# A hybrid decoder layer: the embedding's projection dealt to three handovers, low weights behind the last addition, fewer sums, seven end tiles by TensorE

## The chip, the cores and the metric

The kernel runs on one core of a Trainium2 chip. The metric is the device time of one execution in microseconds (us). A profiled execution also gives a span, from its first to its last instruction, to which all times of a timeline refer.

The engines are named as the profile names them: PE is TensorE (PEld its weight loads), DVE is VectorE, ACT is ScalarE, POOL is GpSimd, and SP is SyncE, whose queue issues all DMAs here.

## The reference

One layer of a decoder is computed for 256 prompt tokens and 8 single-token samples, all in 32-bit floating point, with model width 2048 and feed-forward width 5632:

```python
h = h + 0.5 * rmsnorm(swiglu(rmsnorm(h, g1), w1_gate, w1_up, w1_down), g1_post)
mix, cb, xb, hs = token_mixer(rmsnorm(h, g_mix), ...)     # w_in -> conv group | SSD group -> w_out
h = h + rmsnorm(mix, g_mix_post)
h = h + 0.5 * rmsnorm(swiglu(rmsnorm(h, g2), w2_gate, w2_up, w2_down), g2_post)
gate = sigmoid(rmsnorm(h, g_ple) @ w_ple_gate)
h = h + rmsnorm(gate * (p @ w_ple_proj), g_ple_post)
```

`rmsnorm(x, g)` is `x * rsqrt(mean(x*x) + 1e-6) * g`. The token mixer has an input projection, a conv group (1024 channels, 31 taps), an SSD group (48 heads, 8 groups, state 128) and an output projection. The product `p @ w_ple_proj`, with `p` of width 256, does not depend on `h`; it is called the embedding's projection here.

## The kernel before, in words

**Layout.** Activations lie transposed: 128 channels on the partitions, T = 264 columns (256 prompt, 8 samples) along them. The width 2048 is 16 such tiles (KD). A weight block is 128x128.

**Products.** One 32-bit product is made of three matmuls in a shorter format (`mm3`, L277 to L279): high weights by the high part of the activation, high weights by its low part, low weights by its high part. So each activation tile is split in a high part (written by ACT) and a low part (DVE: value minus high part; tile `act`). Each weight half unit of up to 8 blocks comes by one DMA from SP (`wraw`), is cast by ACT (`whi`, L172), and its rest is taken by DVE (`wlo`, L175). There are 4 buffers of each. A table, `PLAN`, lists the weight units in the order of use; `Weights.next` loads two units ahead of the one in use (`AHEAD`), and a unit has one or two halves.

**Stages in order.** FFN 1; handover 1; the in-projection and the mixer; the out-projection; handover 2; FFN 2; handover 3; the gate's GEMM of the embedding; the tail. A handover is the stretch between the last matmul of one stage and the first of the next: the last output tile is added to its sum (`y`, 16 tiles), squared, and the squares are summed over channels by a matmul with ones (L339, tile `ps`); ACT makes the reciprocal root by Ln and Exp (`rr`); DVE updates `h` tile by tile (`residual`) and splits each into the next stage's input. The squares of the first 14 tiles or so are added up along the way in a tile `run`, the last ones go into TensorE by themselves (`SumSq`, `direct` says how many).

**First GEMM of a stage** (`gemm_first`): to start while the input is still being made, 7 or 8 output columns are accumulated side by side, one input tile after another. The first seven matmuls of an input tile need its high part alone. The later columns are done one by one (`gemm_one`).

**Handover 1** issues the embedding's projection: 16 output columns of two blocks each, 96 matmuls, in two weight units; ACT copies each column out (`pp`, L615) and SP stores it in DRAM (`pproj`), from where the last stage loads it. Handovers 2 and 3 issue `HANDOVER = (4, 11)` matmuls on an identity whose result is not used (`warm`, L379): 4 ahead of the last sum and 11 behind it.

**Handover 1's extra sums.** There the norm of the updated `h` is taken before `h` exists, from three sums: of y squared, of h times y (`hy`) and of y squared with gains (`yy`).

**The mixer** sends scan values through DRAM: `rows` to `d_bc`, and back as `cbc`, broadcast over the partitions; DVE multiplies the sample states with `cbc` (L241).

**The tail** makes `h + e * scale` for the 16 tiles: five tiles by TensorE (identity times h, plus identity times the scaled e, copied by ACT), four by POOL, the rest by DVE, and stores them.

**Order.** A scheduler orders the instructions of each engine; `tc.high_priority`, `tc.issue_after` and `tc.keep_in_program_order` bind it. Engines take their instructions in that order. The diff's lines in the code after are numbered otherwise: L277 to L279 become L302 to L304, L339 becomes L363, L241 and L244 become L266 and L269, L175 becomes L185.

## Time and profile before

| | us |
|---|---|
| median of 3 runs (lowest to highest) | 2396.03 (2394.15 to 2398.36) |
| the profiled execution | 2395.91 |
| its span | 2394.1 |
| PE busy | 2365.5 |
| DVE busy | 1579.9 |
| ACT busy | 1185.8 |
| FFN 1 ends, handover 1 begins (PE) | 769.8 |
| out-projection ends, handover 2 begins | 1513.4 |
| FFN 2 ends, handover 3 begins | 2281.2 |
| last matmul of the gate's GEMM | 2379.8 |

The granted TensorE clock was 0.996 over the span. A timeline row reads: start, duration, engine, line, operation, output tile and inputs, shape, count, and in brackets how long the engine had been idle and what released it. Rows of like instructions that follow each other are drawn together ("x8"), with the duration of the whole group. A matmul on 32-bit operands (the sums, the warm ones) leaves two records. A window row has us, busy time and count of PE, PEld, DVE, ACT and POOL, the granted clock, the DMA share and GB/s.

### The profile page before, as it was taken

The page shows a single profiled execution, that of the slowest core. Times are in us where ns is not written, and L with a number is a line of the kernel's source. Part 1 is how long each engine was busy: PE and PEld are TensorE (multiplying, and loading weights), DVE is VectorE, ACT ScalarE, POOL GpSimd, SP SyncE. Part 2 cuts the span into 40 slices and gives each one's busy share as a digit, 9 for nine tenths or more (in the row PEclk, how much of TensorE's full clock was granted, in tenths as well). Part 3 has the DMA queues.
Part 4 walks back from the last instruction along what each step waited for, and adds up shares of the span by engine and source line. Part 5 has one row for each costly group of instructions (what it writes and reads, how often), then busy time and mean ns, then how long its engine had stood idle before and what let it go on. Part 6 is the DMA issues. An engine that isn't in the chain of part 4 may idle for free.

```text
span 2394.1 us, 47473 instructions
## 1 busy us (share of the span) xinstructions
PE 2365.5 (99%) x19540; PEld 2345.8 (98%) x19540; DVE 1579.9 (66%) x2380; ACT 1185.8 (50%) x1786; POOL 183.3 (8%) x201
## 2 busy tenths in 40 slices
PE   9999999999999989999999999999999999999998
PEld 9999999999999988999999999999999999999998
DVE  7554455545557978989898965866545665565586
ACT  6444444434456565566665455644444443344465
POOL 1400000000004000000000021010100000000103
PEclk9999999999999999999999999999999999999999
DMA  7665555565556766666665556467666676666563
GB/s 259 217 185 184 183 182 183 185 183 182 183 172 190 261 212 203 212 218 216 221 215 175 184 175 230 160 229 242 233 212 227 237 235 220 217 229 214 180 206 134
DMA packets 163434, 489.89 MB, mean 205 GB/s; under 512 B 25312, under 2 KB 43024, under 8 KB 163216
## 3 DMA queue, kind: packets, MB, share of 16 engines
q1 hardware_dynamic: 163216, 486.85, 62.8%
q8 instruction: 153, 2.51, 0.4%
q14 instruction: 65, 0.53, 0.1%
HBM read 465.65 MB, written 22.42 MB: 204 GB/s over the span
## 4 chain that ended last, share of the span: by engine, by line
PE 92%; DVE 3%; DMA 2%; issue 1%; ACT 1%; SPq 0%; POOL 0%; ACTq 0%; DVEq 0%; POOLq 0%
PE acc L277 29%; PE acc L279 29%; PE acc L278 29%; PE ps L277 1%; PE ps L278 1%; DVE wlo L175 1%; PE ps L279 1%; DMA d_bc<-rows 1%; DMA cbc<-d_bc 1%; ACT whi L172 1%; DMA wraw<-in_w 1%; DVE h L241 0%; PE ps L339 0%; DVE h L244 0%; PE ps L880 0%
## 5 line engine op out<-in xcount | busy, mean ns | idle before, releaser
L279 PE MATMUL acc<-act,wlo 128*128 128x264 f32 x6128 | 1735.5, 285 | 7.9 <-DVE wlo L175 7.8
L278 PE MATMUL acc<-act,whi 128*128 128x264 f32 x6128 | 1721.2, 282 | 0.0
L277 PE MATMUL acc<-act,whi 128*128 128x264 f32 x6128 | 1705.7, 282 | 7.6 <-DVE h L244 4.3
L175 DVE TENSOR_TENSOR wlo<-wraw,whi 128x1024 fp32r<-128x1024 f32 (+2 forms) x814 | 977.6, 1203 | 576.4 <-ACT whi L172 574.3
L172 ACT CAST whi<-wraw 128x1024 fp32r<-128x1024 f32 (+2 forms) x814 | 832.0, 1024 | 970.9 <-PE acc L278 689.5
L277 PEld LDWEIGHTS acc<-act,whi 128*128 128x128 f32 x6128 | 1149.9, 189 | 10.7 <-DVE h L244 4.4
L279 PEld LDWEIGHTS acc<-act,wlo 128*128 128x128 f32 x6128 | 1146.8, 187 | 10.7 <-DVE wlo L175 9.4
L278 PEld LDWEIGHTS acc<-act,whi 128*128 128x128 f32 x6128 | 1148.9, 187 | 1.5 <-issue 0.5
L241 POOL TENSOR_TENSOR run<-run,tmp 128x264 f32<-128x264 f32 x77 | 72.3, 939 | 887.3 <-ACT tmp L268 886.8
L244 DVE SCALAR_TENSOR_TENSOR y<-v,vec,y 128x255 f32<-128x255 f32 (+26 forms) x240 | 107.6, 471 | 0.7
L241 POOL TENSOR_TENSOR s<-s,eap 128x1024 f32<-128x1024 f32 x24 | 49.1, 2046 | 626.7 <-DMA s<-in_hst 554.0
L244 DVE SCALAR_TENSOR_TENSOR s<-bb,xds,s 128x128 f32<-128x128 f32 x192 | 52.6, 346 | 59.9 <-POOL s L241 59.9
L241 DVE TENSOR_TENSOR tmp<-acc,rr 128x264 f32<-128x264 f32 x99 | 42.5, 430 | 50.7 <-PE acc L279 50.7
L286 ACT CAST act<-tmp 128x264 fp32r<-128x264 f32 x104 | 42.0, 411 | 53.1 <-DVE tmp L241 51.4
L241 DVE TENSOR_TENSOR tmp<-tmp,acc 128x264 f32<-128x264 f32 x84 | 35.9, 428 | 40.0 <-PE acc L279 39.5
L241 POOL TENSOR_TENSOR run<-run,y 128x264 f32<-128x264 f32 x7 | 9.5, 1350 | 590.3 <-ACT run L321 514.5
L241 DVE TENSOR_TENSOR act<-tmp,act 128x264 fp32r<-128x264 f32 x120 | 54.2, 455 | 0.5 <-ACT act L286 0.5
L278 PE MATMUL ps<-act,whi 128*128 128x264 f32 x192 | 52.3, 283 | 0.0
L279 PE MATMUL ps<-act,wlo 128*128 128x264 f32 x192 | 52.1, 284 | 0.0
L268 ACT ACTIVATE tmp<-tmp 128x264 f32<-128x264 f32 x112 | 47.0, 420 | 7.3 <-DVE tmp L241 7.0
L268 ACT ACTIVATE tmp<-y 128x264 f32<-128x264 f32 x67 | 28.0, 425 | 44.6 <-DVE y L241 43.3
L241 DVE TENSOR_TENSOR y<-y,acc 128x264 f32<-128x264 f32 x80 | 34.0, 425 | 23.9 <-PE acc L279 23.8
(172 smaller groups left out, 1037.6 us busy)
## 6 DMA issues: line engine op xcount, KB each, us to landing
wraw<-in_w SPq DMA_DIRECT2D x755, 512.0 KB
h<-in_hst SPq DMA_DIRECT2D x24, 512.0 KB
s<-in_hst SPq DMA_DIRECT2D x24, 512.0 KB
out_nss<-s SPq DMA_DIRECT2D x24, 512.0 KB
wraw<-in_w SPq DMA_DIRECT2D x35, 256.0 KB
wraw<-in_w SPq DMA_DIRECT2D x23, 384.0 KB
ab<-d_cs SPq DMA_DIRECT2D x16, 384.0 KB
cbc<-d_bc SPq DMA_DIRECT2D x8, 512.0 KB
```

The costliest lines, as they stand in the source:

```text
L172: self.hi = nc.scalar.copy(hi[:, c:d], raw[:, c:d]).ins
L175: nc.vector.tensor_tensor(out=lo[:, c:d], in0=raw[:, c:d], in1=hi[:, c:d].bitcast(F32), op=ALU.subtract)
L241: return (eng or nc.vector).tensor_tensor(out=out, in0=in0, in1=in1, op=op)
L244: return nc.vector.scalar_tensor_tensor(out=out, in0=in0, scalar=scalar, in1=in1, op0=op0, op1=op1)
L268: i = nc.scalar.activation(out=out, in_=in_, func=func, bias=bias, scale=scale)
L277: nc.tensor.matmul(acc, hi, x[:, 0, :], start=first, stop=False)
L278: nc.tensor.matmul(acc, hi, x[:, 1, :], start=False, stop=False)
L279: traced[0] = nc.tensor.matmul(acc, lo, x[:, 0, :], start=False, stop=last).ins
L286: nc.scalar.copy(t[:, 0, :], x)
```

## The change

1. The embedding's 16 columns are dealt out by `PP = (8, 12)`: 8 at handover 1, 4 at handover 2, 4 at handover 3, each as one weight unit of the plan. They are issued in a fixed order with the sums: one column between the sum of `run` and the last sum, the others behind it. The warm matmuls of the handovers are gone. `p` is loaded and split again for handovers 2 and 3. The last four columns are copied straight to the tiles where they are used; 12 go through DRAM.
2. Low weights: some subtractions are deferred (`defer`, `later`) and issued later (`flush`): the second half of the next stage's first unit behind the last addition, its second unit behind the second residual and behind a split inside `update_input` (`load_late`).
3. Six sums (L339) fewer: a constant is added into `run`, and three `SumSq` give no square to TensorE by itself. The sum of a first GEMM is pinned ahead of its last input tile.
4. The first input tile of the stages behind handovers 2 and 3 is made from y with the product of two gains (`both`), high and low part on DVE; h's first tile is updated later.
5. `hy` and `yy` take the gain as a factor, so y need not be scaled first.
6. In the tail seven tiles go by TensorE, the last DVE pair is done as single tiles, stores are by pair, and the first three identity products stand between the two sums.

```diff
-HANDOVER = (4, 11)
+PP = (8, 12)
...
+    def embed(lo, hi):
+        plan.append(("pp", [0, 1], list(range(lo, hi))))
...
-    for q in range(2):
-        plan.append(("pp", [0, 1], list(range(8 * q, 8 * q + 8))))
+    embed(0, PP[0])
...
+    embed(PP[0], PP[1])
     ffn(2)
+    embed(PP[1], KD)
...
+                    def low(lo=lo[:, c:d], raw=raw[:, c:d], hi=hi[:, c:d]):
+                        self.lo = keep(
+                            nc.vector.tensor_tensor(out=lo, in0=raw, in1=hi.bitcast(F32), op=ALU.subtract)
+                        ).ins
+
+                    if a >= defer:
+                        self.later.append(low)
+                        continue
...
+    def flush(self, behind):
+        with self.tc.issue_after(behind), self.tc.high_priority(offset=1000):
+            self.later.popleft()()
+
+    def load_late(self, after):
+        self.after = after
+        self.load(defer=0)
+        self.after = None
...
-        def total(self, behind=None, idle=(0, 0)):
-            d = ps_tile([P, P]) if idle[0] else None
+        def total(self, behind=None, keep=lambda ins: ins, between=None):
             p = ps_tile([P, T])
             with tc.issue_after(behind) if behind is not None else nullcontext():
                 for i, s in enumerate(self.parts):
                     last = i == len(self.parts) - 1
-                    if last and idle[0]:
-                        warm(idle[0], d)
-                    m = nc.tensor.matmul(p, ones, s, start=i == 0, stop=last)
-            if idle[1]:
-                tc.keep_in_program_order(m)
-                warm(idle[1], d)
+                    if last and between:
+                        between()
+                    keep(nc.tensor.matmul(p, ones, s, start=i == 0, stop=last))
...
+                    if m == KD - 1 and ws.later:
+                        ws.flush(i.ins)
                     done(m, ys[m])
+                    if m == 2:
+                        ysq.add_plain(eq)
...
+    def embed(lo, hi, out, **how):
+        w = ws.next(**how)
+        for m in range(lo, hi):
+            acc = acc_tile()
+            for i in range(2):
+                mm3(acc, w[i * (hi - lo) + m - lo], pacts[i], i == 0, i == 1, tc.keep_in_program_order)
+            out(m, acc)
+            yield m
+
+    def ysq_total(ysq, cols):
+        return ysq.total(traced[0], tc.keep_in_program_order, lambda: next(cols))
...
-    ysq, hy, yy = (SumSq(KD, f"run{i}", ep, urgent=not i) for i in range(3))
+    ysq, hy, yy = (
+        SumSq(n, f"run{i}", ep, urgent=not i, direct=d) for i, n, d in ((0, KD + 1, 1), (1, KD, 0), (2, KD, 1))
+    )
...
-        tt(t, H(m), y, ALU.mult)
+        stt(t, y, gain, H(m), ALU.mult, ALU.mult)
...
-    def update_input(rs, post, pre):
-        xs, sq = [], SumSq(KD, eng=nc.vector)
+    def update_input(rs, stage):
+        post, pre = GAINS[stage]
+        xs, sq, made = [], SumSq(KD, eng=nc.vector, direct=0), []
         with tc.high_priority():
-            for k in range(5):
-                if k < 4:
-                    residual(k, ys[k], rs, post, tc.keep_in_program_order)
-                if k:
-                    xs.append(split(H(k - 1), V(pre, k - 1), tc.keep_in_program_order))
+            t, x, u = tmp(), act_tile(), tmp()
+            keep_order(stt(t, ys[0], both[:, stage : stage + 1], rs, ALU.mult, ALU.mult))
+            keep_order(stt(x[:, 0, :], H(0), V(pre), t, ALU.mult, ALU.add))
+            keep_order(stt(u, H(0), V(pre), t, ALU.mult, ALU.add))
+            keep_order(tt(x[:, 1, :], u, x[:, 0, :].bitcast(F32), ALU.subtract))
+            xs.append(x)
+            for k in range(1, 5):
+                residual(k % 4, ys[k % 4], rs, post, lambda i: made.append(keep_order(i).ins))
+                if k == 2:
+                    ws.flush(made[-1])
+                if k > 1:
+                    xs.append(split(H(k - 1), V(pre, k - 1), lambda i: made.append(keep_order(i).ins)))
+                if k == 3:
+                    ws.flush(made[-1])
...
+    cols = embed(PP[1], KD, lambda m, acc: nc.scalar.copy(e4[m // 4][:, m % 4, :], acc), fill=False)
+    rs = ffn_scale(ysq, cols)
+    ws.load_late(order["last"])
+    for _ in cols:
+        pass
+    xs, sq = update_input(rs, 1)
...
-TAIL_VECTOR = [(0, 2), (2, 1), (3, 1), (4, 2), (6, 2), (8, 2), (10, 2)]
-TAIL_TENSOR = [0, 1, 2, 4, 5]
+TAIL_VECTOR = [(0, 2), (2, 1), (3, 1), (4, 2), (6, 2), (8, 2), (10, 1), (11, 1)]
+TAIL_TENSOR = [0, 1, 2, 4, 5, 6, 7]
```

Where instructions stand, first on VectorE at handover 3. `wlo_0` and `wlo_8` are the two halves of a weight unit's low part, `y` the last addition, `act` the low part of an input tile. Before:

```order
L241 TENSOR_TENSOR y_21725<-y_21725,acc_27354 128x264
L175 TENSOR_TENSOR wlo_8_27363<-wraw_8_27361,whi_8_27362 128x768
L175 TENSOR_TENSOR wlo_0_27410<-wraw_0_27408,whi_0_27409 128x1024
L241 TENSOR_TENSOR y_21788<-y_21788,acc_27407 128x264
L175 TENSOR_TENSOR wlo_8_27416<-wraw_8_27414,whi_8_27415 128x768
L244 SCALAR_TENSOR_TENSOR tmp_27483<-y_20819,vec,rr_27460 128x264
L241 TENSOR_TENSOR h_17895<-h_17895,tmp_27483 128x264
L244 SCALAR_TENSOR_TENSOR tmp_27486<-y_20882,vec,rr_27460 128x264
L241 TENSOR_TENSOR h_17895<-h_17895,tmp_27486 128x264
L244 SCALAR_TENSOR_TENSOR act_27489<-h_17895,vec,act_27489 128x264
```

The same place in the change (the first unit's halves are 27370 and 27376, the second unit's 27443 and 27448):

```order
L185 TENSOR_TENSOR wlo_0_27370<-wraw_0_27368,whi_0_27369 128x1024
L266 TENSOR_TENSOR y_21745<-y_21745,acc_27367 128x264
L185 TENSOR_TENSOR wlo_8_27376<-wraw_8_27374,whi_8_27375 128x768
L269 SCALAR_TENSOR_TENSOR tmp_27475<-y_20776,both,rr_27427 128x264
L269 SCALAR_TENSOR_TENSOR act_27476<-h_17814,vec,tmp_27475 128x264
L269 SCALAR_TENSOR_TENSOR tmp_27477<-h_17814,vec,tmp_27475 128x264
L266 TENSOR_TENSOR act_27476<-tmp_27477,act_27476 128x264
...
L185 TENSOR_TENSOR wlo_0_27443<-wraw_0_27441,whi_0_27442 128x1024
L269 SCALAR_TENSOR_TENSOR act_27489<-h_17814,vec,act_27489 128x264
...
L185 TENSOR_TENSOR wlo_8_27448<-wraw_8_27446,whi_8_27447 128x768
```

The second unit's low weights stood ahead of the last addition and behind it, all before the first tile; now the first unit's stand there, and the second unit's are among the input tiles.

Second, TensorE at handover 1 in the change: the end of the FFN (`acc_8959`), then sums and embedding columns (`acc_9016`, `acc_9069`):

```order
L304 MATMUL acc_8959<-act_8055,wlo_8_8848 128x264
L363 MATMUL ps_9014<-run_8108,ones 128x264
L302 MATMUL acc_9016<-act_9007,whi_0_8901 128x264
...
L304 MATMUL acc_9016<-act_9010,wlo_8_8908 128x264
L363 MATMUL ps_9014<-tmp_8997,ones 128x264
L363 MATMUL ps_9030<-run_8114,ones 128x264
L363 MATMUL ps_9030<-tmp_9002,ones 128x264
L363 MATMUL ps_9033<-run_8112,ones 128x264
L302 MATMUL acc_9069<-act_9007,whi_0_8901 128x264
```

Before, the six sums were spread among the columns; now five stand close together around the first column.

Third, VectorE in the mixer's first group. Before, two low-weight subtractions stood ahead of the two `cbc` products:

```order
L175 TENSOR_TENSOR wlo_0_10164<-wraw_0_10162,whi_0_10163 128x1024
...
L175 TENSOR_TENSOR wlo_8_10170<-wraw_8_10168,whi_8_10169 128x1024
...
L241 TENSOR_TENSOR h_478_9922<-h_478_9922,cbc_9920 128x1024
L241 TENSOR_TENSOR h_479_9924<-h_479_9924,cbc_9920 128x1024
```

In the change one of the two stands behind them:

```order
L185 TENSOR_TENSOR wlo_0_10083<-wraw_0_10081,whi_0_10082 128x1024
...
L266 TENSOR_TENSOR h_466_9841<-h_466_9841,cbc_9839 128x1024
L266 TENSOR_TENSOR h_467_9843<-h_467_9843,cbc_9839 128x1024
L185 TENSOR_TENSOR wlo_8_10089<-wraw_8_10087,whi_8_10088 128x1024
```

The second half of a weight unit moved behind the products that wait for `cbc`.

167 lines of the change are left out of this document (90 added, 77 removed).

## The prediction

> **What bounds the kernel now.** I read the page first (busy shares and the clock row), then the waits of TensorE, then timelines of TensorE, VectorE and ScalarE around the three handovers, the mixer's first group and the tail.
>
> ```profile
> PE 2365.5 (99%) x19540; PEld 2345.8 (98%) x19540; DVE 1579.9 (66%) x2380; ACT 1185.8 (50%) x1786; POOL 183.3 (8%) x201
> PE acc L279 <- DVE wlo L175: 7.8, 6, 4.2
> PE acc L277 <- DVE h L244: 4.3, 1, 4.3
> PE acc L277 <- ACT whi L172: 3.0, 3, 2.5
> 1517.20:1552.80 35.60, 35.40 (x296) 35.21 (x295) 35.39 (x73) 23.22 (x44) 0.00 (x0) 1.00 0.50 161
> ```
>
> TensorE is busy 99%, so what it issues is what the kernel costs. The window row (us, then busy and records of PE, PEld, DVE, ACT, POOL, then clock) gives the price: 35.6 / 296 = 0.120 us per matmul. It also holds the trap: in that window, which is the first GEMM after handover 2, VectorE is busy 35.39 of 35.6 us. There a matmul saved is worth nothing if VectorE is later. Only about 24 us of the span are TensorE waits; the waits rows name the largest, all in the mixer.
>
> **Handover 1.** Today all 16 embedding columns (96 matmuls) stand there.
>
> ```profile
> 769.75 0.28 PE L279 MATMUL acc<-act,wlo 128*128 128x264 f32 x1
> 771.78 0.71 PE L339 MATMUL ps<-run,ones 128*128 128x264 f32 x2 [0.22 <-POOL run L241]
> 770.65 1.98 POOL L241 TENSOR_TENSOR run<-run,tmp 128x264 f32<-128x264 f32 x2 [2.09 <-ACT tmp L268]
> 772.59 1.79 POOL L241 TENSOR_TENSOR run<-run,hy 128x264 f32<-128x264 f32 x1
> 783.44 0.43 DVE L241 TENSOR_TENSOR act<-tmp,act 128x264 fp32r<-128x264 f32 x1
> 786.26 0.43 DVE L241 TENSOR_TENSOR act<-tmp,act 128x264 fp32r<-128x264 f32 x1
> 770.00:785.50 15.50, 14.94 (x109) 13.93 (x108) 11.42 (x19) 13.07 (x31) 3.73 (x3) 1.00 0.73 244
> ```
>
> The last FFN matmul starts at 769.75; the window is filled with 109 records until 785.5, where the in-projection effectively begins. The change leaves 8 columns there: 48 x 0.12 = 5.76 us go. Its order now puts the sum of run directly behind the last FFN matmul. That sum waits for POOL as it does today (771.78), with nothing in front, so TensorE idles 1.9 us. Then one column (0.72), and the sums of tmp, yy and hy in a fixed order. The last of these can start when POOL's hy addition ends, 772.59 + 1.79 = 774.4. It costs 0.44 us (below), seven columns 42 x 0.12 = 5.04: 779.9. The first input column is then ready, so the in-projection starts near 780.1 in place of 785.5: **-5.4 us**. VectorE makes one input column every 786.26 - 783.44 = 2.82 us there, TensorE uses one in 24 x 0.12 = 2.88. The lead shrinks but does not vanish. If it did, 16 tiles at a little over 2.88 would cost up to 1 us; if the sums' waits hide better, 0.5 more is won: between -4.4 and -5.9.
>
> **Handovers 2 and 3.** Each loses 15 warm matmuls and gets four columns, 24 x 0.12 = 2.88 us.
>
> ```profile
> 1513.42 0.29 PE L279 MATMUL acc<-act,wlo 128*128 128x264 f32 x1
> 1513.55 0.61 PE L339 MATMUL ps<-run,ones 128*128 128x264 f32 x2
> 1513.99 1.05 PE L379 MATMUL ps<-ident,ones 128*128 128x128 f32 x8
> 1514.45 0.42 DVE L241 TENSOR_TENSOR y<-y,acc 128x264 f32<-128x264 f32 x1
> 1515.44 0.71 PE L339 MATMUL ps<-tmp,ones 128*128 128x264 f32 x2 [0.40 <-ACT tmp L268]
> 1515.99 2.62 PE L379 MATMUL ps<-ident,ones 128*128 128x128 f32 x22
> 1517.24 0.49 DVE L244 SCALAR_TENSOR_TENSOR tmp<-y,vec,rr 128x264 f32<-128x264 f32 x1 [1.50 <-ACT rr L268]
> 1518.81 0.51 PE L277 MATMUL acc<-act,whi 128*128 128x264 f32 x2 [0.20 <-ACT act L268]
> 1560.72 0.39 PE L277 MATMUL ps<-act,whi 128*128 128x264 f32 x1 [0.42 <-DVE rr L421]
> ```
>
> A sum costs 1513.99 - 1513.55 = 0.44 us. The last matmul starts at 1513.42, but the addition that needs it waits for a low-weight subtraction and starts at 1514.45. In the change that subtraction stands behind the addition, which then starts a third of a us behind the last matmul (its 0.29 and the signal), near 1513.75: 0.7 us. The first input tile now comes from VectorE alone (two of its instructions, then the tile is there) instead of two on VectorE and one on ScalarE (1517.24 to 1518.81): 0.55 us more. The columns (2.88) and both sums (0.88) fit under this chain. The GEMM starts near 1517.6, **1.2 us earlier**; handover 3 shows the same steps:
>
> ```profile
> 2281.21 0.29 PE L279 MATMUL acc<-act,wlo 128*128 128x264 f32 x1
> 2282.24 0.42 DVE L241 TENSOR_TENSOR y<-y,acc 128x264 f32<-128x264 f32 x1
> 2284.93 0.49 DVE L244 SCALAR_TENSOR_TENSOR tmp<-y,vec,rr 128x264 f32<-128x264 f32 x1 [1.40 <-ACT rr L268]
> 2286.49 0.51 PE L277 MATMUL acc<-act,whi 128*128 128x264 f32 x2
> 2291.35 0.49 DVE L244 SCALAR_TENSOR_TENSOR tmp<-y,vec,rr 128x264 f32<-128x264 f32 x1
> 2291.76 1.22 DVE L175 TENSOR_TENSOR wlo<-wraw,whi 128x1024 fp32r<-128x1024 f32 x1
> 2292.89 0.43 DVE L241 TENSOR_TENSOR run<-run,tmp 128x264 f32<-128x264 f32 x1
> 2293.24 0.49 DVE L244 SCALAR_TENSOR_TENSOR tmp<-y,vec,rr 128x264 f32<-128x264 f32 x1
> 2294.79 0.95 DVE L175 TENSOR_TENSOR wlo<-wraw,whi 128x768 fp32r<-128x768 f32 x1
> 2295.66 0.43 DVE L241 TENSOR_TENSOR run<-run,tmp 128x264 f32<-128x264 f32 x1
> 2326.32 0.61 PE L339 MATMUL ps<-run,ones 128*128 128x264 f32 x2
> ```
>
> The GEMM starts near 2285.2 instead of 2286.49 (-1.3). But then VectorE, already full, gets more to do: the embedding's unit takes a place of the two-unit lookahead, so both halves of the second unit's low weights (two subtractions) and the extra operations of the first tile land inside its chain. Start to start the rows give 0.405 (scalar_tensor_tensor, 2291.35 to 2291.76), 1.13 (1024 wide), 0.35 (tensor_tensor, 2292.89 to 2293.24) and 0.87 (768 wide, 2294.79 to 2295.66). In the new order the low half of the fifth input tile is VectorE's 29th instruction, at either handover: 15 x 0.405 + 9 x 0.345 + 3 x 1.135 + 2 x 0.87 = 14.3 us after the chain's start, today's 1517.24 (2284.93) less the 0.7 = 1516.55 (2284.24), hence at 1531.0 (2298.7). TensorE, 7 columns x 3 x 0.12 = 2.52 us per tile, asks for it after four tiles and the seven matmuls that need only the high half: 1517.6 + 10.08 + 0.84 = 1528.5 (2296.1). So it **stalls 2.5 us**, and 0.2 more at the next tile; the later tiles catch up. One sum of the two at the end of this GEMM goes (0.44). Handover 2: 1517.6 + 16 x 2.52 + 0.44 + 2.7 = 1561.0, against 1560.72, and the constant that column 7 waits for today (0.42 in its row) comes no earlier, since its ScalarE work stands behind a weight cast; with 1 us for that it is **+1.3**, between -2.4 (no stall) and +2.1. Handover 3: 2285.2 + 40.32 + 0.44 + 2.7 = 2328.7, against 2286.49 + 40.32 + 0.88 = 2327.7: **+1.0**, between -1.7 and +2.
>
> **Fewer sums.** Two are gone in the first FFN, one in the second, on TensorE's path and with nothing waiting: 3 x 0.44 = **-1.3**. The others (hy, the two behind update_input) are in the figures above.
>
> **The mixer** is untouched in code, but the scheduler's order moved.
>
> ```profile
> 861.78 0.85 SPq L826 DMA_DIRECT2D cbc<-d_bc  x1
> 869.18 2.36 DVE L241 TENSOR_TENSOR h<-h,cbc 128x1024 f32<-128x1024 f32 x2 [4.61 <-DMA cbc<-d_bc]
> 876.25 0.59 PE L279 MATMUL acc<-act,wlo 128*128 128x264 f32 x1 [4.19 <-DVE wlo L175]
> 872.00:876.20 4.20, 0.06 (x1) 0.00 (x0) 4.20 (x7) 0.79 (x1) 0.00 (x0) 0.52 0.39 123
> 876.20:878.00 1.80, 1.75 (x8) 1.75 (x9) 1.80 (x3) 1.30 (x2) 0.00 (x0) 0.50 0.73 259
> 878.00:880.00 2.00, 2.00 (x11) 2.00 (x11) 2.00 (x5) 1.99 (x5) 0.00 (x0) 0.50 0.74 297
> ```
>
> VectorE stands at the cbc products 4.61 us for their DMA, and low weights queue behind. In the change one more half unit of low weights stands behind them (its 1.13 us and the products' 2.36 come ahead of a tile that TensorE needs sooner), but one weight load of 512 KB less is ahead of the DMA chain that feeds cbc. If cbc lands 2.5 us earlier, TensorE resumes about 1 us earlier than 876.25; if it lands as today, 1.5 us later. The seven later groups have smaller shifts. I take **0**, between -3 and +4.
>
> The stall of 4.19 us is followed by a granted clock of 0.50 (last two rows): a long stall is paid twice. The Trainium skill states this rule ("TensorE: Matmul & The Clock Gate", Part 1: after about 3.4 us without work TensorE runs at half rate until it has been busy as long again), and this trace agrees with its 0.50. By that rule taking the warm matmuls away speaks against the change; the idle that I count in the handovers (1.9 us at most) and the 2.5 us stalls are shorter than the 4.19 that is seen to do it, so the sum has no such loss, and it is a rival below.
>
> **Tail.**
>
> ```profile
> 2389.86 0.70 DVE L241 TENSOR_TENSOR h<-h,prod 128x528 f32<-128x528 f32 x1
> 2388.07 2.88 SPq L1186 DMA_DIRECT2D out_y<-h  x6
> ```
>
> The chain sum, Ln, Exp, products stays. VectorE's list gets two tiles shorter and its last two pairs become single tiles; at the 0.43 of a single tile's addition it ends some 0.5 us before today's 2389.86 + 0.70 = 2390.56, and the last store is half as large, but stores queue on SP (six in 2.88 us). **-0.3**, between -0.6 and +0.2.
>
> **Sum.** -5.4 + 1.3 + 1.0 - 1.3 + 0 - 0.3 = -4.7 us. The profiled execution took 2395.9 (span 2394.1 and 1.8 around it), 0.1 below the median of 2396.03; so 2391.2 to 2391.3, and I say **2391.2 us**. A change under 0.2%, 4.8 us, cannot be told from none here; the forecast lies on that border.
>
> **The rivals.**
> (a) VectorE keeps up in both GEMMs: the stalls fall away. For it: later tiles have slack, and a stall on TensorE also delays the casts. Against it: 35.39 of 35.6 us busy today. It gives 2391.2 - 2 x 2.7 = 2386 us. Chance 0.25.
> (b) The handover's gain is spent again: the in-projection becomes bound by VectorE. Its 2.82 us against 2.88 leave 0.06 a tile; If the weight casts, which share ScalarE with these tiles, come 0.3 us later per tile, 16 tiles cost about 4.5: 2395.7. Chance 0.15.
> (c) On the other side: the cbc products, moved ahead of low weights in all eight groups. From the point where cbc is not earlier than today, each group holds TensorE for one more subtraction, 1.13 us, and in the first one longer: 8 x 1.13 + 1 = 10: 2401.3 us, slower. For it: the waits row of 7.8 us on low weights shows that path live. Against it: the DMA chain is shorter. Chance 0.08.
> (d) The clock halves in handovers 2 and 3. A half-rate stretch as long as the one seen (876.2 to 880 and a little more) loses about 2 us each: 2391.2 + 4 = 2395.2. Chance 0.04.
> The forecast with its own range, 2388.5 to 2394.5, keeps 0.48; half of that lies below 2391.2.
>
> **The numbers.** Faster by over 0.2%: all of (a) and half of the forecast, 0.25 + 0.24 = 0.49. Slower by over 0.2%: (c) and a little of (b), 0.10. The rest, 0.41, is within 0.2%. The range goes from full gain, 2385.5, to just over (b) and (d), 2397: one in ten is left out above, less below.
>
> **What would show it.** TensorE's first in-projection matmul about 10.3 us behind the last FFN matmul, where 15.75 lie today; a wait of 2 to 3 us of TensorE for VectorE's input tiles (act) near 14 us after the start of each VectorE chain, where today there is none; first GEMMs that start 4.1 us behind the last matmul in place of 5.4; no half-rate clock in the handovers; the wait on cbc in the first group within 2.5 us of 4.61. The forecast is wrong if that act wait is missing, if the in-projection's first GEMM shows waits for VectorE, or if the mixer's stalls sum to more than 4 us away from today's.

## The result, and the profile after

The changed kernel took **2403.86 us** (median of 9 runs, 2400.64 to 2408.05), the kernel before on the same chip 2397.3 (9 runs, 2394.15 to 2399.92): a ratio of 1.0028, 95% interval 1.0018 to 1.0038. It is **slower by 0.28%**, where 2391.2 us was forecast; 2403.86 lies outside the range. Its profiled execution is the fastest of the nine: 2400.64 us, span 2398.9, against 2395.91 and 2394.1 before. The profiles of two experiments below (the state term first, and the products later) fell on disturbed executions and are not read.

The table gives stretches of TensorE's timeline, cut at the start of the first or last matmul of each. (In the kernel before, six matmuls of the embedding stand among the first ones of the in-projection, which begin at 784.78; there the cut is put at 785.51, so that the first GEMM has its own 384 matmuls as in the other columns.) "Again" is a second profile of the changed kernel; the last four columns are experiments told below.

| us | before | after | again | padded | sixteen | three edits | among sums |
|---|---|---|---|---|---|---|---|
| FFN 1 | 769.75 | 769.05 | 768.58 | 768.48 | 770.15 | 768.74 | 768.65 |
| handover 1 | 15.76 | 9.30 | 9.36 | 15.45 | 17.40 | 17.32 | 16.32 |
| first GEMM of the in-projection | 45.96 | 47.19 | 47.11 | 46.06 | 45.96 | 45.96 | 46.17 |
| rest of in-projection, mixer, out-projection | 681.95 | 684.76 | 687.72 | 682.82 | 677.34 | 675.00 | 677.60 |
| handover 2 | 5.38 | 4.20 | 4.20 | 4.20 | 4.94 | 4.94 | 4.94 |
| first GEMM of FFN 2 | 41.21 | 44.03 | 44.07 | 44.02 | 41.96 | 42.02 | 41.98 |
| up to column 7 | 0.70 | 2.10 | 2.09 | 2.09 | 2.09 | 1.23 | 1.24 |
| rest of FFN 2 | 720.49 | 722.49 | 723.48 | 721.38 | 721.64 | 720.03 | 720.03 |
| handover 3 | 5.28 | 4.11 | 4.10 | 4.10 | 4.94 | 4.94 | 4.94 |
| first GEMM of the gate | 41.21 | 44.08 | 45.41 | 45.43 | 41.94 | 41.95 | 41.93 |
| rest of the gate | 52.09 | 53.18 | 52.72 | 51.84 | 53.18 | 52.72 | 52.72 |
| tail | 14.32 | 14.44 | 16.13 | 14.59 | 16.62 | 14.33 | 14.34 |

Handover 1 gave 6.46 us and handovers 2 and 3 gave 1.2 each, and more than all of it was lost in the stretches behind them. First the page of the changed kernel and the waits of its TensorE (us in total, times, longest):

```profile
PE 2364.3 (99%) x19476; PEld 2342.3 (98%) x19476; DVE 1577.8 (66%) x2394; ACT 1186.6 (49%) x1790; POOL 185.1 (8%) x206
```

```profile
PE acc L304 <- DVE wlo L185: 9.9, 5, 7.3
PE ps L930 <- DVE xde L266: 3.8, 2, 2.4
PE acc L303 <- DVE act L269: 3.8, 4, 1.6
PE acc L302 <- DVE h L269: 3.3, 1, 3.3
PE ps L302 <- DVE rr L442: 1.8, 1, 1.8
```

TensorE issues 64 records less and is busy 1.2 us less, yet the span is 4.8 longer. Three rows are new or much larger: `act` is the stall that was forecast for the two GEMMs, `rr` is column 7's constant (0.4 us before), and `xde` is a wait in the mixer that the prediction did not name (0.7 us in the kernel before). The row of `wlo` holds one wait of 7.3 us, where the longest was 4.2.

Handover 1 on TensorE (last FFN matmul, first sum, the last sums, first input column):

```profile
769.05 0.29 PE L304 MATMUL acc<-act,wlo 128*128 128x264 f32 x1
770.06 0.71 PE L363 MATMUL ps<-run,ones 128*128 128x264 f32 x2 [0.72 <-POOL run L266]
...
772.72 0.71 PE L363 MATMUL ps<-run,ones 128*128 128x264 f32 x2
...
778.35 0.28 PE L302 MATMUL acc<-act,whi 128*128 128x264 f32 x1
```

From 769.05 to 778.35 are 9.30 us. The first sum waits 0.72 us and not the 1.9 of the forecast.

The mixer's first group (near 865) and second group (near 935): VectorE, then TensorE, then three windows of TensorE's clock (PEclk, the third number from the end):

```profile
863.79 2.36 DVE L266 TENSOR_TENSOR h<-h,cbc 128x1024 f32<-128x1024 f32 x2 [7.99 <-DMA cbc<-d_bc]
866.07 1.22 DVE L185 TENSOR_TENSOR wlo<-wraw,whi 128x1024 fp32r<-128x1024 f32 x1
...
933.04 1.22 DVE L185 TENSOR_TENSOR wlo<-wraw,whi 128x1024 fp32r<-128x1024 f32 x1
934.18 0.55 DVE L266 TENSOR_TENSOR xde<-xdt,dte 128x384 f32<-128x384 f32 x1
934.65 1.22 DVE L185 TENSOR_TENSOR wlo<-wraw,whi 128x1024 fp32r<-128x1024 f32 x1
...
936.54 0.55 DVE L266 TENSOR_TENSOR xde<-xdt,dte 128x384 f32<-128x384 f32 x1
```

```profile
867.34 0.59 PE L304 MATMUL acc<-act,wlo 128*128 128x264 f32 x1 [7.30 <-DVE wlo L185]
...
934.88 0.88 PE L930 MATMUL ps<-xde,rr 128*128 128x384 f32 x2 [2.37 <-DVE xde L266]
937.24 1.62 PE L930 MATMUL ps<-xde,rr 128*128 128x384 f32 x2 [1.48 <-DVE xde L266]
```

```profile
867.00:871.00 4.00, 3.66 (x16) 3.66 (x17) 4.00 (x9) 0.65 (x1) 0.00 (x0) 0.50 0.48 136
903.00:909.00 6.00, 3.53 (x16) 3.54 (x17) 6.00 (x21) 3.00 (x11) 0.00 (x0) 0.50 0.77 249
935.00:941.00 6.00, 4.52 (x23) 2.63 (x24) 4.64 (x10) 2.22 (x6) 0.00 (x0) 0.72 0.71 226
```

VectorE stands 7.99 us for `cbc`, where it stood 4.61, and the half of low weights that TensorE needs is the next instruction behind it. TensorE resumes 88.99 us after the in-projection's start (867.34 less 778.35); before it was 876.25 less 785.5, 90.75, so this stall by itself lost nothing. The `xde` waits near 935 did: up to there the two kernels run even, behind them the changed one is 5 us later by the starts of equal matmuls. The same two instructions of VectorE, and TensorE's one wait for them, in the kernel before:

```profile
937.00 0.55 DVE L241 TENSOR_TENSOR xde<-xdt,dte 128x384 f32<-128x384 f32 x1
...
940.32 0.56 DVE L241 TENSOR_TENSOR xde<-xdt,dte 128x384 f32<-128x384 f32 x1
```

```profile
PE ps L880 <- DVE xde L241: 0.7, 1, 0.7
```

TensorE comes to the first of these products 154 us behind the in-projection's start in both kernels. VectorE starts its input after 151.5 us before (937.00 less 785.51) and after 155.8 us now (934.18 less 778.35), because the `cbc` products start 1.7 us later behind the in-projection's start (863.79 less 778.35, where it was 869.18 less 785.51), and from them up to it VectorE has 20 subtractions of low weights in its queue instead of 18, and 123 instructions instead of 115. Each long wait has a stretch at half the clock behind it, but in sum these stretches are alike: from 800 to 1000 us the granted clock is 0.96 in both kernels.

Handover 2: the fifth input tile and column 7 on TensorE, VectorE ahead of column 7, then windows.

```profile
1528.49 0.39 PE L303 MATMUL acc<-act,whi 128*128 128x264 f32 x1 [1.55 <-DVE act L269]
...
1560.62 0.39 PE L302 MATMUL ps<-act,whi 128*128 128x264 f32 x1 [1.81 <-DVE rr L442]
```

```profile
1559.00 1.23 DVE L185 TENSOR_TENSOR wlo<-wraw,whi 128x1024 fp32r<-128x1024 f32 x1 [3.06 <-ACT whi L181]
1560.14 0.43 DVE L442 TENSOR_SCALAR rr<-ps 128x264 f32<-128x264 f32 x1
```

```profile
1515.80:1555.00 39.20, 37.26 (x303) 36.44 (x302) 38.56 (x76) 25.21 (x46) 0.00 (x0) 1.00 0.56 182
1558.00:1561.00 3.00, 1.19 (x9) 0.91 (x8) 2.00 (x3) 2.98 (x5) 0.00 (x0) 1.00 0.78 287
1561.00:1564.00 3.00, 3.00 (x19) 3.00 (x18) 2.25 (x5) 2.09 (x4) 0.13 (x1) 0.61 1.01 356
```

VectorE is busy 38.56 of 39.2 us in the first GEMM, and the `act` stall stands within 1 us of where it was forecast. At column 7 the constant stands behind one subtraction of low weights whose cast came late; TensorE waits 1.81 us for it (2.10 from matmul to matmul) and then runs three us at a clock of 0.61.

### The profile page after: what moved, and what is told of

Read it like the earlier page. It is cut to its first block, busy times and chain, and to the rows that moved or that the text cites. A ratio compares the mean times of both kernels' runs of the same rounds, so it can differ in the third digit from the quotient of the medians.

```text
span 2398.9 us, 47334 instructions
## 1 busy us (share of the span) xinstructions
PE 2364.3 (99%) x19476; PEld 2342.3 (98%) x19476; DVE 1577.8 (66%) x2394; ACT 1186.6 (49%) x1790; POOL 185.1 (8%) x206
## 4 chain that ended last, share of the span: by engine, by line
PE 88%; DVE 6%; DMA 3%; issue 2%; ACT 1%; SPq 0%; POOL 0%; DVEq 0%; ACTq 0%; POOLq 0%
PE acc L303 28%; PE acc L304 28%; PE acc L302 28%; DVE wlo L185 2%; DMA wraw<-in_w 1%; DMA cbc<-d_bc 1%; DVE h L266 1%; DMA d_bc<-rows 1%; PE ps L302 1%; PE ps L303 1%; PE ps L304 1%; ACT whi L181 0%; DVE h L269 0%; PE ps L363 0%; DMA s<-in_hst 0%
## 5 line engine op out<-in xcount | busy, mean ns | idle before, releaser
L303 PE MATMUL ps<-act,whi 128*128 128x264 f32 x192 | 52.8, 286 | 0.0
L302 PE MATMUL ps<-act,whi 128*128 128x264 f32 x192 | 46.9, 286 | 2.4 <-DVE rr L442 1.8
```

What stands on the lines that cost most here:

```text
L302: keep(nc.tensor.matmul(acc, hi, x[:, 0, :], start=first, stop=False))
L303: keep(nc.tensor.matmul(acc, hi, x[:, 1, :], start=False, stop=False))
```

## The experiments

Each ratio is to runs of the kernel before on the same chip, side by side with the experiment (its medians lay between 2395.51 and 2397.05).

### The low halves of the second unit by GpSimd

```diff
-    nc.vector.tensor_tensor(out=lo, in0=raw, in1=hi.bitcast(F32), op=ALU.subtract)
+    eng.tensor_tensor(...)        # GpSimd for the two halves issued late at handovers 2 and 3
```

> The changed kernel, but the second weight unit's low halves of the stages behind handovers 2 and 3 (two subtractions, 1024 and 768 wide, at each) are made by GpSimd, which is idle there, instead of VectorE; nothing else. Theory A (VectorE has more to do than TensorE leaves time for, and these two subtractions, 2.0 us, are what the change put into its chain): TensorE's wait for the low half of the fifth input tile (1.83 and 1.84 us in the changed kernel, 3.2 us with the smaller ones around it) falls under 0.8 us at each place, and the kernel gets 4 to 6 us faster than the change (about 2398 to 2400 on the scale where the change takes 2403.9). Rival B (the tiles are late because of ScalarE, its high halves and weight casts): the waits stay within 0.5 us of what they are. Rival C (GpSimd and VectorE get in each other's way in memory): VectorE's instructions there become longer by 2 us in sum, and nothing is won.

Measured: 2411.38 us, ratio 1.0064 (1.0049 to 1.0079). Timelines of VectorE and GpSimd and TensorE's waits in the first GEMM of FFN 2:

```profile
1520.08 2.62 DVE L269 SCALAR_TENSOR_TENSOR tmp<-h,vec,tmp 128x264 f32<-128x264 f32 x1
1522.73 1.92 DVE L266 TENSOR_TENSOR act<-tmp,act 128x264 fp32r<-128x264 f32 x1
```

```profile
1520.04 4.31 POOL L185 TENSOR_TENSOR wlo<-wraw,whi 128x1024 fp32r<-128x1024 f32 x2 [4.74 <-ACT whi L181]
```

```profile
PE acc L303 <- DVE act L266: 3.5, 1, 3.5
```

The stall at the fifth tile is gone and a longer one stands at the first. Two VectorE instructions of 0.49 and 0.43 us take 2.62 and 1.92 while GpSimd subtracts. The Trainium skill states this in "SBUF — State Buffer" ("Who interferes with whom"): VectorE, with two inputs in SBUF, and a GpSimd instruction that reads SBUF exclude each other for a whole instruction. This trace agrees with its 2.62 and 1.92 us. Behind the wait of 3.5 us TensorE ran at half clock, and each of the two first GEMMs took 3.4 us more than in the changed kernel's first profile. Another 6.1 us of this execution lie in the mixer (690.84), where the order of instructions is the changed kernel's; the edit does not explain them.

### The state term ahead of two subtractions

```diff
+            if c == 0 and ws.later:
+                ws.flush(made_xde.ins)      # one unit's low halves behind the first xde of the second group
+                ws.flush(made_xde.ins)
```

> The changed kernel, but in the mixer one weight unit (that of the second group's last x column) has its low halves made behind the first xde product of the second group instead of ahead of it; the scheduler orders the rest anew. In the changed kernel in-projection and mixer take 731.9 us from first to last matmul against 727.9 before, and TensorE waits 3.8 us in two pieces for xde there, with half the clock behind it. Theory D (the 4 us of the mixer are this one wait: xde queues on VectorE behind low weights): the wait on xde falls under 1 us and the stretch to 727 to 728 us, so the kernel is 4 to 5 us faster than the change. Rival E (the mixer takes what the scheduler's order happens to give, and any new order moves it by a few us either way): the wait on xde goes, but other waits come up, and the stretch lies anywhere from 726 to 736 us.

Measured: 2412.57 us, ratio 1.0068 (1.0051 to 1.0085). That is some 9 us above the changed kernel, where D forecast 4 to 5 below it. Without a profile it isn't shown whether the `xde` wait went, nor where the time was lost.

### Sixteen columns at the first handover

```diff
-PP = (8, 12)
+PP = (8, 16)        # all columns at handover 1; 4 and 11 warm matmuls back at handovers 2 and 3; no late unit
```

> The changed kernel with the dealing undone: all 16 embedding columns stand at handover 1 again, in two weight units, and handovers 2 and 3 have warm matmuls (4 and 11) as before; fewer sums, first tile by VectorE, the tail and the deferred second half of a weight unit stay. Theory A (the dealt unit takes a place of the lookahead and so pushes low weights into VectorE's chain): TensorE's waits for input tiles behind handovers 2 and 3 fall under 0.8 us each, column 7's waits fall back to under 1 us with no half clock behind it, handover 1 gets 5.8 us longer. In sum, leaving the mixer out, 4 to 5 us under the kernel before; the mixer, whose order moves again, adds between -4 and +4. Rival F (the first tile by VectorE alone, which stays, is what makes the tiles late): waits of 2 us and more at the fifth tile stay.

Measured: 2397.15 us, ratio 1.0003 (0.9994 to 1.0012): with the dealing undone the change is no longer slower. Handover 1 pays for it with 8.1 us (17.40 after 9.30), more than the 5.8 that theory A took. In the table the two first GEMMs fall by 2.1 us each (44.03 to 41.96), so three quarters of their 2.8 us over the kernel before go with the dealing and its late unit on VectorE, a quarter stays with the rest of the change. TensorE's wait at the fifth tile falls from 1.55 to 0.8 us, as A said and not F. Column 7 keeps its 2.09, where A had under 1 us of waiting. And the mixer's stretch, in a new order, is 677.34, 7.4 us under the changed kernel and 4.6 under the kernel before: without it the dealing gains more than it loses, by the other rows of the table.

### The kernel before without its warm matmuls

```diff
-HANDOVER = (4, 11)
+HANDOVER = (0, 0)
```

> The kernel before with no warm matmuls in handovers 2 and 3, so that TensorE stands idle there for about 1.4 and 3 us around the sum of 0.44 us. Theory G (an idle of that length costs the clock): the granted clock falls to half for 3 us or so behind one or both handovers, and each such stretch loses 1.5 to 2.5 us; 2 to 5 us slower than before. Rival H (the pieces of idle are too short, as the 1.83 us stalls of the changed kernel behind handovers 2 and 3, which show a clock of 1.00): no change, within 1 us.

Measured: 2398.71 us, ratio 1.0012 (1.0002 to 1.0021). Timeline of TensorE and a window:

```profile
1515.32 0.71 PE L339 MATMUL ps<-tmp,ones 128*128 128x264 f32 x2 [1.29 <-ACT tmp L268]
1518.68 1.47 PE L277 MATMUL acc<-act,whi 128*128 128x264 f32 x5 [2.65 <-ACT act L268]
```

```profile
1518.80:1521.00 2.20, 2.20 (x10) 2.20 (x11) 2.17 (x7) 1.88 (x5) 0.00 (x0) 0.50 0.07 23
```

Waits of 1.29 and 2.65 us, apart by one sum, bring a clock of 0.50, and the two GEMMs take 43.85 and 42.82 us instead of 41.21. Without the warm matmuls the kernel is 0.12% slower; in the changed kernel the four columns do that service, and no half clock stands in its handovers 2 and 3 themselves.

### The tail of before

```diff
-TAIL_TENSOR = [0, 1, 2, 4, 5, 6, 7]
+TAIL_TENSOR = [0, 1, 2, 4, 5]        # and stores by single tile, first additions behind the sum
```

> Edit: the changed kernel with the tail of the kernel before: five end tiles by TensorE instead of seven, each stored alone, and their first additions begun behind the sum over the columns. Nothing ahead of the tail is touched. Theory I (the tail now depends on the clock): in the changed kernel's own profile the tail took 14.44 us, but 16.12 and 16.62 in the profiles of the two experiments that keep its seven tiles, where TensorE's 32-bit products ran at about 0.65 us instead of 0.39; with five tiles the tail should be 14.3 us whatever the clock, and the median 1 to 2 us below that of the changed kernel (2403.86), so near 2402.3. Theory J (the seven tiles cost nothing on the whole; the spread of the changed kernel comes from the mixer): the tail is again 14.3 us, as before, and the median stays within 0.5 us of 2403.9.

Measured: 2401.98 us, ratio 1.0027 (1.0017 to 1.0037), which cannot be told from the changed kernel's 1.0028. The traces say more. With five tiles the tail is 14.3 to 14.4 us in all seven profiles that have them; with seven tiles it is 14.4 to 14.6 in three and 16.1 to 16.6 in four. A window of TensorE in the tail, 5.5 and 6.2 us behind its start, in the changed kernel's two profiles:

```profile
2390.00:2392.00 2.00, 2.00 (x11) 1.71 (x10) 2.00 (x4) 1.09 (x3) 1.92 (x3) 1.00 0.37 130
```

```profile
2395.00:2397.00 2.00, 2.00 (x6) 1.49 (x6) 1.97 (x4) 0.76 (x2) 2.00 (x2) 0.50 0.38 137
```

Eleven records in 2 us, or six at half clock. So theory I holds in the profiles (some 1.8 us in four of seven), and its share of the median is too small for these runs.

### The constant by ScalarE

```diff
-nc.vector.tensor_scalar(out=eq, in0=p, scalar1=EPS / P, scalar2=EPS * EPS * DM / P, op0=ALU.mult, op1=ALU.add)
+act(eq, p, AF.Identity, bias=eps2, scale=EPS / P)
```

> Edit: the constant that the pinned sum adds for the rounding term (eq) is made by ScalarE, as an Identity with scale and bias right behind the logarithm, and no longer by VectorE, where it stands behind a subtraction of low weights. The rest of the changed kernel stays. Theory K (column 7's wait is that constant's place in VectorE's queue): the wait of 2.10 us at column 7 of the second handover falls to about 1.2 us, the stretch of half clock behind it (1561.7 to 1565 us) goes, because the idle time ahead of it is shorter, and the median is 0.9 to 2.4 us lower than the changed kernel's, near 2402. Theory L (the wait is the logarithm behind a cast on ScalarE, and the half clock would come anyhow): column 7 waits 1.8 to 2.1 us as before, FFN 2 keeps its 722.5 us, and the median stays at 2403.9.

Measured: 2404.06 us, ratio 1.0033 (1.002 to 1.0045). Waits at that place, and the windows around it:

```profile
PE ps L302 <- ACT rr L293: 1.0, 1, 1.0
```

```profile
1560.00:1563.00 3.00, 2.05 (x16) 1.77 (x15) 1.22 (x1) 2.45 (x4) 0.00 (x0) 1.00 0.97 294
1563.00:1566.00 3.00, 3.00 (x27) 3.00 (x26) 2.19 (x4) 2.83 (x5) 0.00 (x0) 1.00 0.96 363
```

K's mechanism is shown: the step to column 7 falls from 2.10 to 1.24 us, here and in the four later profiles with this edit, no half clock follows in any of them, and the rest of FFN 2 takes 721.14 instead of 722.49. (In the padded kernel, whose clock stayed full behind the step of 2.09, it took 721.38.) The median shows nothing of it: in this execution the first GEMM of the in-projection took 48.44 (47.19), the mixer's stretch 686.28 (684.76) and the tail 16.13.

### The changed kernel again

> Edit: none; the changed kernel once more, for a second trace. Theory M (the mixer's 2.8 us is what executions differ by): with every engine's order equal, the stretch from the first in-projection product to the second handover differs from its 684.76 us by 2 us or more, with other gaps in other places, while the first GEMMs behind the second and third handovers repeat their 44.0 and 44.1 us within 0.3. Theory N (the mixer's loss is in the program: the embedding term behind two low-weight subtractions on VectorE): the stretch is 684.8 within 1 us, with the same gap of about 2.6 us ahead of the group's first normalised tile near 929 us.

Measured: 2406.68 us in one run. M holds as to size: with the same order on every engine the mixer's stretch is 687.72, 3.0 us more. But the `xde` gaps from matmul to matmul, 2.65 and 1.96 us, are there again to the hundredth, so N has the place right: they belong to the program, and what differs between executions adds to them. The GEMM behind handover 3 took 45.41, not within 0.3 of 44.08. The stall at its fifth input tile and the three us behind it, in the first profile, then in this one:

```profile
2301.21 0.39 PE L303 MATMUL acc<-act,whi 128*128 128x264 f32 x1 [1.56 <-DVE act L269]
2302.00:2305.00 3.00, 3.00 (x25) 2.90 (x25) 3.00 (x8) 1.74 (x5) 0.00 (x0) 1.00 0.66 203
```

```profile
2304.71 0.39 PE L303 MATMUL acc<-act,whi 128*128 128x264 f32 x1 [1.54 <-DVE act L269]
2305.00:2308.00 3.00, 3.00 (x17) 3.00 (x17) 3.00 (x7) 1.58 (x5) 0.00 (x0) 0.54 0.59 194
```

The wait is the same, and once the clock is 1.00 behind it, once 0.54.

Three experiments (the low halves by GpSimd, the tail of before, the constant by ScalarE) leave the order of the mixer's instructions as it is in the changed kernel on all four engines. Their stretches there are 690.84, 686.47 and 686.28. So one order gives 684.8 to 690.8 us in five profiles, all above the order before (681.95, and 681.84 without the warm matmuls).

### Three edits

```diff
-PP = (8, 12)
+PP = (8, 16)        # with the tail of before and the constant by ScalarE
```

> Edit: three edits in one: all sixteen columns at the first handover with the warming products back behind the other two (as in the experiment that undoes the dealing), the tail of the kernel before, and the constant by ScalarE. What stays of the change: the low weights behind the last addition, the first tile made by VectorE, and the fewer sums. By the theories I and K the undealt kernel's median of 2397.15 should lose 1 to 2 us in the tail and 1 to 2 in column 7, so 2393 to 2395, 1 to 3 us under the kernel before on the same chip. By J and L it stays at 2397, with no difference from before.

Measured: 2393.56 us, ratio 0.9992 (0.9983 to 1.0001): 10 us under the changed kernel by the medians, some 9 by the ratios, and just not to be told from the kernel before. The mixer's stretch is 675.00, in the order of the sixteen columns (677.34).

### The first group's products later

```diff
-            if j >= late:
-                state_times_c(g, j - late)      # at the x tiles of the first two groups
+            if g == 1:                          # at the B tile of the second group
+                state_times_c(0, 0)
+                load_state(0, 2)
+                state_times_c(0, 1)
```

> Edit: the changed kernel with the cbc products of the mixer's first group issued one to two column tiles later (when the next group's B and first x tile are done, instead of at the first group's x tiles), so that they stand behind the low weights that TensorE needs next; the first group's sample part and gate and the second group's cbc load and products move with them. In the changed kernel's own profile VectorE stands 7.99 us at the first cbc product while the low weights that TensorE needs wait behind it, and TensorE stands 7.58 us from 859.76 on and runs at half clock to about 871. Theory P (that wait is what the mixer loses by): VectorE has work in those 8 us, TensorE's stall at 860 falls below 2 us with no half clock behind it, the later wait at the embedded state term near 932 (2.65 and 1.96 us) shrinks too because VectorE is ahead, and the mixer's stretch falls from 684.8 to 687.7 down to 674 to 680; the median is 7 to 12 us under 2403.9. Theory Q (VectorE's sum of work in that group sets the pace, the wait only moves): a stall of 5 us or more appears at the next group's products or at the state term, the stretch stays above 683, and the median within 3 us of 2403.9.

> Edit: the kernel of the three edits (all columns at the first handover, the tail of before, the constant by ScalarE) with the same later cbc products in addition. There the stalls of the first group are 1.54 and 3.91 us near 867 to 875 and 2.91 us near 930, with VectorE waiting about 4.4 us for cbc. By P: 3 to 7 us less than the 2393.56 of the three edits, 2387 to 2391, which beats both kernels. By Q: 2393 within 2 us.

Measured: on the changed kernel 2399.76 us, ratio 1.0009 (0.9999 to 1.0019); on the three edits 2398.1, ratio 1.0007 (0.9998 to 1.0016). By the ratios the first is 4.5 us better than the changed kernel, where P said 7 to 12; the second is 3.6 worse than the three edits, outside what P and Q said. The profile of the second, VectorE's and TensorE's waits:

```profile
DVE h L266 <- DMA cbc<-d_bc: 2.0, 1, 2.0
```

```profile
PE ps L930 <- DVE xde L266: 4.8, 2, 2.6
```

VectorE's wait for `cbc` fell from 3.56 to 2.0 us, and TensorE's longest wait for low weights from 3.6 to 2.6; near 940 TensorE waited 4.8 us for `xde`, for which the three edits had no wait, and came out some 5 us behind. There the stall moved (Q). That the first gained by filling VectorE's 8 us (P) is not shown, since its profile is not read.

### The state's inputs by GpSimd

```diff
-tt(t, xdt[c], dte[...], ALU.mult)
+tt(t, xdt[c], dte[...], ALU.mult, None if g else nc.gpsimd)
```

> Edit: the changed kernel with one operation moved: in the mixer's first group, the two decayed inputs of the state (xde, 128x384 each) are made by GpSimd, which has nothing to do there, instead of VectorE, where each stands behind low-weight subtractions. Every later group keeps VectorE. Theory R (that place in VectorE's queue is where the mixer's loss against the kernel before comes from): TensorE's waits of 2.65 and 1.96 us at the state products near 932 fall to 1 us in all, no half clock follows, and the mixer's stretch loses 3 to 6 us of its 684.8 to 687.7; the median goes from 2403.9 to 2398 to 2401. A GpSimd product of this size is not in the trace; by its 1942 ns for 1024 columns, about 0.8 us, so it is no bound. Theory S (VectorE's sum of work sets the pace, or GpSimd holds VectorE up as it did with the low halves): another stall of the same size appears within 30 us, and the median stays within 2 us of 2403.9.

> Edit: the kernel of the four edits (all columns at the first handover, the tail of before, the constant by ScalarE, the first group's cbc products later) with the two decayed inputs of the first group by GpSimd as well. In that kernel VectorE's wait for cbc had fallen to 2.0 us, TensorE was 3.5 us ahead behind it, and lost more than that again at the state products (waits of 2.47 and 3.10 us near 937 to 940, 4.8 us in the waits rows, and half clock). By R the gain stays: 5 to 9 us under its 2398.1, 2389 to 2393, 4 to 8 us under the kernel before. By S: within 2 us of 2398.

Measured: on the changed kernel 2400.59 us, ratio 1.002 (1.0011 to 1.0029); on the four edits 2395.46, ratio 1.0 (0.9991 to 1.0009). The first one's waits of TensorE:

```profile
PE acc L302 <- DVE b L269: 2.8, 1, 2.8
```

The edit moves the `xde` of the first group, near 885 us, for which TensorE did not wait; the waits near 935 belong to the second group, whose `xde` stays on VectorE. In the new order that the scheduler made, these waits are gone all the same, and a wait of 2.8 us for another VectorE instruction, `b`, stands in their place; the mixer's stretch is 684.33. By the ratios the two kernels are 1.9 and 1.7 us faster than those without the edit, with intervals that overlap. So neither R nor S is decided.

### A padded handover, and columns among the sums

```diff
+    pad = ps_tile([P, P])
+    warm(28, pad)        # behind the eight columns of handover 1 in the changed kernel
```

> Edit: the changed kernel with 28 matmuls on an identity, whose result is not used, behind the eight columns of the first handover, so that the in-projection starts about as late as in the kernel before. Nothing else is edited; the scheduler's order of the mixer moves by itself: the half of low weights that had gone behind the first group's cbc products stands ahead of them again. Theory T (the six us won at the first handover are given back in the mixer, by the order that the scheduler makes for an earlier start): the handover takes 15 to 17 us instead of 9.3, the mixer's stretch falls from 684.8 to 687.7 to 677 to 682, and the median stays within 2.5 us of 2403.9. Theory U (the mixer's loss has nothing to do with the handover's length): the stretch stays at 684 to 688, and the median rises by 6 to 7 us, to 2410.

Measured: 2402.34 us, ratio 1.0028 (1.0019 to 1.0037): the same ratio as the changed kernel's, though its first handover is 6.15 us longer (15.45); the first GEMM fell by 1.1 to 46.06 and the mixer's stretch to 682.82, 1.9 to 4.9 under the two profiles of the changed kernel. VectorE in the first group:

```profile
856.85 1.23 DVE L185 TENSOR_TENSOR wlo<-wraw,whi 128x1024 fp32r<-128x1024 f32 x1 [0.51 <-ACT whi L181]
...
866.77 2.36 DVE L266 TENSOR_TENSOR h<-h,cbc 128x1024 f32<-128x1024 f32 x2 [4.01 <-DMA cbc<-d_bc]
```

The low half stands ahead of the products again, and their wait is 4.01 us instead of 7.99. T has the median and the moved order right, and U falls. But the stretch misses T's 677 to 682. Of the 6.15 us, 3.1 come back by the end of the out-projection against the changed kernel's first profile, and 6.0 against its second. The second group's `xde` waits are still there:

```profile
PE ps L932 <- DVE xde L266: 3.2, 2, 2.6
```

```diff
-    rs = ffn_scale(ysq, cols)
+    next(cols)                          # one column ahead of the first sum, on top of the three edits
+    rs = ffn_scale(ysq, cols, 3)        # three between the sums of run and tmp; one more ahead of the last sum
```

> Edit: the kernel of the three edits (all columns at the first handover, the tail of before, the constant by ScalarE) with the first handover's columns placed among its sums: one ahead of the first sum, three instead of one behind it, and one between the last two sums. The order of the mixer stays the same but for a few instructions of its second group. Theory V (TensorE idles 0.7, 1.4 and 0.7 us between those sums, which stand in a fixed order with one column among them, and the columns fill it): the handover falls from 17.3 to 14.3 to 15 us, below the 15.76 of the kernel before, and the median goes from 2393.56 to about 2391, some 5 us under the kernel before. Theory W (the columns ahead of the sums delay the chain to the first input tile by as much): the handover stays at 17, the median at 2393.5.

Measured: **2393.32 us, ratio 0.9985 (0.9976 to 0.9994)**, faster than both kernels. The sum of `tmp` in the timeline of the three edits, the same sum here, and the wait that is new here:

```profile
772.57 0.71 PE L363 MATMUL ps<-tmp,ones 128*128 128x264 f32 x2 [1.39 <-ACT tmp L293]
```

```profile
772.49 0.71 PE L363 MATMUL ps<-tmp,ones 128*128 128x264 f32 x2
```

```profile
PE acc L302 <- ACT pp L609: 1.1, 2, 0.6
```

The columns fill the wait, but each needs an accumulator that ScalarE has still to copy out, so the handover gains 1.0 us (16.32) and not three; the median moved by 0.2, and most of what makes this kernel faster was there with the three edits.

## Why the prediction was wrong

**Handover 1, -5.4: right in size, in part by luck.** It gave -6.46, since the first sum waited 0.72 us where 1.9 was forecast, and the first GEMM behind it took 1.23 back (one wait of 0.84 us for an input's low part, a sign of being wrong in the prediction's own list), -5.2 in all. What failed is the claim that this gain reaches the end: the padded kernel gives it up and has the same ratio.

**The mixer, 0 between -3 and +4: wrong, the largest miss.** It cost 2.8 us in the changed kernel's first profile, 5.8 in the second, 4.3 to 8.9 in the three experiments with the same order, and 2.4 and 0.9 in the two that keep the dealing with another order (GpSimd's `xde`, the padded handover). The prediction saw the moved half of low weights and priced it by one wait, and that part came out even. The step that failed is "the seven later groups have smaller shifts", priced at nothing. It did not follow VectorE's queue on into the second group: two more subtractions stand ahead of the `xde` inputs there, and TensorE waits 2.37 and 1.48 us for them, then runs at part of its clock. What was not in the sum either is that an edit to a handover 80 us earlier gives the mixer another order, with its own code untouched: 684.8 to 690.8 us in the changed kernel's order, 682.8 padded, 675.0 to 677.6 with all columns at handover 1. Rival (c) had the sign right and came nearest (2401.3), by a mechanism that was seen in the first group alone, where it cost nothing in sum. No run removes the `xde` waits alone, so their share of the loss is read from the profiles and not shown by an experiment; why a given order comes out good or bad stays open.

**Handover 2, +1.3: the parts right, two sizes off.** The start came 1.2 us earlier, as forecast. The stall of 2.7 us at VectorE's low parts (its sum of 14.3 us gives 1530.9 and not 1531.0, which changes nothing) is there (1.9 us in two waits, the rest in steps between matmuls that are one or two tenths of a us longer): the GEMM grew by 2.82 where 2.7 less a sum, 2.26, was forecast. Column 7 was mis-sized: 1 us was taken, 2.10 came, and the step said its cause was ScalarE's cast alone; the constant then stood behind a subtraction on VectorE as well. And it brought a stretch at part clock of about 1.5 us (thirty matmuls took 5.28 us there; behind the same wait in the GpSimd experiment, at full clock, 3.74).

**Handover 3, +1.0:** the same, +1.70 at the end of its first GEMM (-1.17 and +2.87). The rest of the gate took 1.1 us more, for which there was no term: 0.63 of it is the step to its own column 7 (0.87 us instead of 0.24, with a wait of 0.6 us for ScalarE's `rr`). The other 0.46 is not in the second profile, and its cause stays open.

**Fewer sums, -1.3: right** where it can be read alone (FFN 1 lost 0.70 us with two sums fewer, 1.17 in the second profile, forecast 0.88).

**Tail, -0.3: wrong in kind.** It is +0.1 or +1.8, since seven products put TensorE on its path, and they take twice as long when the clock is halved there.

**The rivals.** (a) fell: VectorE did not keep up. (b) fell: the in-projection's GEMM lost 1.2 us, not 4.5. (d), half clock in handovers 2 and 3, did not come there but came at column 7, in the tail, and in the second profile behind the `act` stall of handover 3, where it cost 1.3 us; "shorter than the 4.19 that is seen to do it" was the faulty step, since waits of 1.81 and 1.54 us did it. The page of the Trainium skill that the prediction names ("TensorE: Matmul & The Clock Gate", Part 1) also says that the gate's window runs freely, so that a transition depends on where in the window the work falls. Column 7, the `act` stall and the tail fit that, with half clock behind the same wait in some profiles and not in others; the Trainium skill's idle time of about 3.4 us does not fit, as these waits were shorter.

Added up in the profiled executions: forecast -4.7, measured +4.8. Of the 9.5 between, the mixer has 2.8, the rest of FFN 2 behind column 7 2.4 (the part clock about 1.5 of it), handover 2 up to column 7 1.7, the rest of the gate 1.1, handover 3 0.7, the tail 0.4, FFN 1 and handover 1 0.35. The median is 3.2 above the profiled execution; the second profile, 6.0 above it, has 3.0 of that in the mixer, 1.7 in the tail and 1.3 in the gate's first GEMM.

## What to carry to other kernels

A gain ahead of a stage whose order a scheduler makes is not a gain until that stage has been read again: compare the order of the whole stage, and follow the queue of the engine that is full there, instruction by instruction, past the first difference. Work that is dealt out to fill idle time has a price at the engine that prepares its weights; here the late unit cost 2.1 us in each of two GEMMs. The dealing took 8.1 us out of handover 1 and 0.7 and 0.8 out of the other two, and the mixer's new order, 7.4 us longer, then tipped the balance. Two profiles of one order differ too: here by up to 6 us in one stage, so a single profile does not price an order. Before a filler or a placeholder is taken away, and before TensorE is put on the path of a tail, price a halved clock for it, also behind waits under 2 us.

## What the runs showed of the hardware that was not expected

- A wait of 1.81 us, in a window of 3 us that was busy for 1.19, was followed by a clock of 0.61. A wait in the middle of a busy stretch was followed by full clock in one profile (1.56 us) and by 0.54 in another of the same kernel (1.54 us). Behind the step of 2.09 to 2.10 us to column 7 thirty matmuls took 5.27 to 5.29 us in five profiles and 3.74 in two.
- In the profiles that are read, the stretches at half clock lasted 3.4, 6.8 or 10.2 us, all but the one that ends each profile. The shortest costs some 1.7 us, an estimate: half of 3.4.
- Three microseconds of tail that TensorE shares with three other engines run at full or half clock from execution to execution (11 or 6 records in 2 us).
- While GpSimd subtracted two halves of low weights (4.31 us together), VectorE instructions with two SBUF inputs took 2.62 us instead of 0.49 and 1.92 instead of 0.43.
